# One Trainium2 core, a hybrid decoder layer: a hand-written TensorE order in which ten pieces of projection work instead of six stand ahead of the triangular solve's first product, and group norms that are issued in pieces

## The chip, the cores and the metric

One kernel runs on one core of a Trainium2 chip. A core has five engines with a queue of instructions each: TensorE (PE, matrix products; its weight loads are listed as PEld), VectorE (DVE), ScalarE (ACT), GpSimd (POOL) and SyncE (SP, which here only starts transfers). Each engine takes its instructions strictly in the order of its queue and waits on semaphores for other engines. The metric is the time of one execution on the device in microseconds (us), lower is better.

## What is computed

One decoder layer over 256 tokens of width 2048: RMSNorm, one input projection, whose columns go to two groups of heads, an output projection with a residual add, then a gated MLP of width 5632 with a causal convolution of three taps, and a final RMSNorm. Cut to what matters here, the two head groups are:

```python
def rwkv7_scan(r, w, k, v, a, b):            # 16 heads of 64, token by token
    sa = jnp.einsum('bhvk,bhk->bhv', state, a_t)
    state = state * w_t + sa[..., None] * b_t + v_t[..., None] * k_t
    out = jnp.einsum('bhvk,bhk->bhv', state, r_t)
...
mu = jnp.mean(y, axis=-1, keepdims=True)     # group norm of a head's 64 values
var = jnp.mean(jnp.square(y - mu), axis=-1, keepdims=True)
y = ((y - mu) * lax.rsqrt(var + GN_EPS)).reshape(bsz, s, c) * gn_w + gn_b
bonus = jnp.sum(r * k * r_k, axis=-1, keepdims=True) * v
return (y + bonus.reshape(bsz, s, c)) * g    # g: the gate
...
sc = q_nope @ k_nope.T + q_pe @ k_pe.T       # 8 attention heads, causal softmax, p @ v
```

## The kernel before

**Weights.** Every weight block of 128x1024 numbers is loaded by SyncE into a `raw` tile, ScalarE copies it to a rounded `hi` (L133) and VectorE writes the rest `lo` = raw - hi (L134); TensorE then multiplies hi by the activations' high and low parts and lo by their high part (`prod_c`, L175 and L178; `prod_a`, L195 to L197). Three buffers of each of raw, hi and lo go round. Accumulators in PSUM come from three rings: `mm` (3), `ch` (3) and `at` (2).

**The scan as a blocked solve.** The token-by-token recurrence is cut into four chunks of 64 tokens. For each head and chunk a triangular system of 64 is inverted by blocks of 32. `gram` (L525) forms the products, and its GpSimd transfers write the 32x32 blocks to a DRAM tile `dL`; `solve_load` (L578) reads them back as `Lp`; `solve` (L582) inverts the blocks on VectorE in 31 steps of a product `tm` (L594) and a sum `Tq` (L596) each, copies the result (`tp`, L598) and sends it by GpSimd transfers through DRAM into the tiles `T11` and `TT` (L604 to L613; the trace writes T11 as `T`). `solve_r` (L639) and `solve_t` (L654) then are 64 small 32x32 products each with the weight tiles T11 and TT; between them VectorE writes `RT`, after them `TT`. `chunk_a`, `chunk_b`, `chunk_c` (L697, L714, L723) do a chunk's products of state, solve and output, with VectorE evictions `XB`, `UV`, `ST` between them; the output lands in `yt`.

**The filling.** `all_units` (L917) is a generator of 30 pieces of projection work for the attention group, called units here: 16 halves of the eight latent tiles (two to a tile, `latent_tile`, L792; VectorE evicts a finished tile as `cr`, L801), then the up-projections (`up_b`, `up_v`). Behind the first latent tile of the second group, and again behind the first of the up-projections, stands a `latent_rs` (L814), which sends its sums `pss` through VectorE (`ssm`) and 14 small GpSimd instructions (`rsqrt`) to `rr`; `bcast` (L232) turns `rr` by two diagonal tiles `dg` and a product `rsb` into a row. `rope_q` (L846) rotates `qr` with a shifted copy `qs`, which four GpSimd transfers write.

**The order around the change.** From L969 on the order of TensorE's instructions is written out by hand (`manual_schedule`): `unit(6)`, `solve_r`, two units, `solve_t`, `chunk_a(0)`, two units, `chunk_b(0)`, a unit, `chunk_c(0)`, and for chunks 1 to 3 a unit before each of the three parts. Then come the eight attention heads: `scores(h)` (L870), the softmax on VectorE and ScalarE, `attend_t(h)` (L899, it waits for the softmaxed tile `pexp`) and `attend(h)` (L908), with the last units, the group norms of the two halves of the tokens (`gn_vec`, L746, `gn_gate`, L768, `gn_out`, L777) and the pieces of the output projection (`out_piece`, L952, 4 column blocks x 4 pieces for each half of the input) between them. The queues of the other engines are not written out: a scheduler places their instructions by its own model of time, and that order is fixed in the program. The rest of the program, from the output projection's second half through the MLP, lies behind that.

## Time and profile before

| what | value |
|---|---|
| runs shown | 6599.56, 1209.99 and 1216.69 us, median 1216.69 |
| the profiled execution | 1211.91 us, of which the span of the profile is 1210.1 us |
| TensorE busy over the span | 1164.1 us (96%) |
| VectorE, ScalarE, GpSimd busy | 815.7, 587.3 and 72.7 us |
| TensorE's mean granted clock | 0.986 |

The span is the time from the first to the last recorded instruction; the 1.8 us around it are not in the rows. A row of a timeline gives start, duration, engine, line, operation, output<-inputs and count; a bracket at its end is the idle time of that engine just before, with what ended it. A row of the waits gives who waited for whom, the total, the number of times and the longest. A row of the windows gives each engine's busy time in a stretch, TensorE's granted clock (1.00 is full) and the share and rate of the DMA engines. An x16 row of L175 or a x8 row of L178 is one half of a latent tile's three products.

### The profile page before, as it was taken

What the parts mean: (1) busy time and instruction counts of PE and PEld (TensorE: products, weight loads), DVE (VectorE), ACT (ScalarE), POOL (GpSimd) and SP (SyncE); (2) the same over time, 40 slices, a digit from 0 to 9 for tenths busy, and PEclk for the clock granted to TensorE, in tenths of its full rate; (3) what the DMA queues carried; (4) which work ended last, traced back from release to release, by engine and by line L of the source; (5) the groups of instructions that cost most, each with busy time, mean ns of one, the idle gap of its engine ahead of it and who ended that gap; (6) DMA issues with size and microseconds to landing.
All of it is one profiled execution on the core that took longest, in us unless ns stands there. A gap on an engine that the chain in (4) does not pass through costs nothing.

```text
span 1210.1 us, 19607 instructions
## 1 busy us (share of the span) xinstructions
PE 1164.1 (96%) x7629; PEld 1025.1 (85%) x7629; DVE 815.7 (67%) x1319; ACT 587.3 (49%) x895; POOL 72.7 (6%) x220
## 2 busy tenths in 40 slices
PE   7999989699998999999999999999999999999996
PEld 7899989598886788888888888888888888888885
DVE  6798669556687666777777776444577777776563
ACT  6684335234454345655555554333455555554442
POOL 1600430211000001000000000000000000000000
PEclk9999999789998999999999999999999999999998
DMA  8544455424332555655555555556655555566672
GB/s 323 201 141 156 132 166 174 134 95 145 122 125 92 187 188 175 194 191 191 191 191 191 191 192 191 190 189 192 205 191 191 191 190 191 190 222 208 209 213 83
DMA packets 61485, 215.90 MB, mean 178 GB/s; under 512 B 7376, under 2 KB 8144, under 8 KB 61392
## 3 DMA queue, kind: packets, MB, share of 16 engines
q1 hardware_dynamic: 58544, 209.22, 52.8%
q0 software_dynamic: 2080, 3.38, 1.0%
q10 hardware_dynamic: 768, 2.05, 0.6%
q8 instruction: 60, 0.98, 0.3%
q14 instruction: 33, 0.27, 0.1%
HBM read 210.48 MB, written 3.41 MB: 177 GB/s over the span
## 4 chain that ended last, share of the span: by engine, by line
PE 93%; DVE 3%; DMA 1%; issue 1%; ACT 1%; POOL 0%; ACTq 0%; SPq 0%; DVEq 0%
PE mm L163 27%; PE mm L166 13%; PE mm L175 12%; PE mm L195 9%; PE mm L197 9%; PE mm L196 9%; PE mm L178 6%; PE pg L538 1%; DVE lo L134 1%; PE px L691 1%; ACT hi L133 1%; PE at L175 1%; DMA raw<-in_win 0%; PE py L691 0%; PE pT L661 0%
## 5 line engine op out<-in xcount | busy, mean ns | idle before, releaser
L134 DVE TENSOR_TENSOR lo<-raw,hi 128x1024 fp32r<-128x1024 f32 x376 | 460.2, 1224 | 298.5 <-ACT hi L133 292.6
L133 ACT CAST hi<-raw 128x1024 fp32r<-128x1024 f32 x376 | 395.0, 1050 | 507.6 <-issue 230.6
L163 PE MATMUL mm<-z,hi 128*128 128x512 f32 x1408 | 351.3, 392 | 0.0
L163 PEld LDWEIGHTS mm<-z,hi 128*128 128x128 f32 x1408 | 251.9, 188 | 43.6
L166 PEld LDWEIGHTS mm<-z,lo 128*128 128x128 f32 x1408 | 188.3, 188 | 14.5
L166 PE MATMUL mm<-z,lo 128*128 128x256 f32 x1408 | 191.5, 278 | 0.0
L175 PE MATMUL mm<-x,hi 128*128 128x256 f32 x1024 | 143.0, 289 | 13.4 <-ACT hi L133 8.2
L175 PEld LDWEIGHTS mm<-x,hi 128*128 128x128 f32 x1024 | 130.7, 194 | 16.4 <-ACT hi L133 8.2
L196 PE MATMUL mm<-lo,hh 128*128 128x512 f32 x336 | 130.7, 389 | 0.0
L197 PE MATMUL mm<-hi,hl 128*128 128x512 f32 x336 | 130.7, 389 | 0.0
L195 PE MATMUL mm<-hi,hh 128*128 128x512 f32 x336 | 119.7, 389 | 0.0
L178 PE MATMUL mm<-x,lo 128*128 128x256 f32 x512 | 74.3, 282 | 0.0
L197 PEld LDWEIGHTS mm<-hi,hl 128*128 128x128 f32 x336 | 63.1, 188 | 13.1
L196 PEld LDWEIGHTS mm<-lo,hh 128*128 128x128 f32 x336 | 63.1, 188 | 13.1
L195 PEld LDWEIGHTS mm<-hi,hh 128*128 128x128 f32 x336 | 63.1, 188 | 13.0
L178 PEld LDWEIGHTS mm<-x,lo 128*128 128x128 f32 x512 | 66.1, 189 | 0.6 <-issue 0.3
L195 PE MATMUL mm<-hi,yhi 128*128 128x512 f32 x128 | 50.6, 403 | 1.3 <-DVE x L961 1.3
L197 PE MATMUL mm<-hi,ylo 128*128 128x512 f32 x128 | 50.5, 394 | 0.7 <-DVE ylo L914 0.7
L196 PE MATMUL mm<-lo,yhi 128*128 128x512 f32 x128 | 50.8, 397 | 0.0
L1098 POOL MEMSET gt<- 128x2 f32 x44 | 4.3, 99 | 577.0 <-DVE hl L1110 573.4
L195 PEld LDWEIGHTS mm<-hi,yhi 128*128 128x128 f32 x128 | 24.3, 190 | 7.8 <-DVE x L961 1.8
L197 PEld LDWEIGHTS mm<-hi,ylo 128*128 128x128 f32 x128 | 24.2, 189 | 6.5 <-DVE ylo L914 1.1
(283 smaller groups left out, 1103.6 us busy)
## 6 DMA issues: line engine op xcount, KB each, us to landing
raw<-in_wgu SPq DMA_DIRECT2D x176, 512.0 KB, 3.3
raw<-in_wdn SPq DMA_DIRECT2D x88, 512.0 KB, 4.2
raw<-in_win SPq DMA_DIRECT2D x70, 512.0 KB, 3.5
raw<-in_wout SPq DMA_DIRECT2D x32, 512.0 KB, 3.4
raw<-in_wuq SPq DMA_DIRECT2D x6, 512.0 KB, 3.3
xraw<-in_xT SPq DMA_DIRECT2D x4, 512.0 KB, 6.3
xt<-in_x SPq DMA_DIRECT2D x4, 512.0 KB, 6.9
raw<-in_wuk SPq DMA_DIRECT2D x4, 512.0 KB, 3.3
```

The lines of the kernel that those rows point to most:

```text
L133: S.copy(hi, raw)
L134: last_lo[0] = V.tensor_tensor(lo, raw, hi.bitcast(F32), ALU.subtract).ins
L163: PE.matmul(acc, hi[:, j * P:(j + 1) * P], act(kt0 + j), start=first and j == 0, stop=False, skip_group_check=True)
L166: PE.matmul(acc[:, :T], lo[:, j * P:(j + 1) * P], act(kt0 + j)[:, 0, :], start=False, stop=last and j == n - 1, skip_group_check=True)
L175: PE.matmul(acc, hi[:, j * P:(j + 1) * P], act(kt0 + j)[:, s, :], start=first and j == 0 and s == 0, stop=False, skip_group_check=True)
L178: PE.matmul(acc, lo[:, j * P:(j + 1) * P], act(kt0 + j)[:, 0, :], start=False, stop=last and j == n - 1, skip_group_check=True)
L195: PE.matmul(accs[tb], ah, wh, start=first and j == 0, stop=False)
L196: PE.matmul(accs[tb], ah, wl, start=False, stop=False)
L197: PE.matmul(accs[tb], al, wh, start=False, stop=last and j == n - 1)
L538: PE.matmul(pg[h][:, o:o + P], BK[pp][hs, gg, w * 2 + r, :, :], AR[pp][hs, gg, w * 2 + r, :, :], start=o == 0, stop=True, skip_group_check ...
L691: PE.matmul(dst[HS[h], a_ * 64:(a_ + 1) * 64], lhsT, rhs, start=first and n == 0 and a_ == 0, stop=True, skip_group_check=True)
L1098: nc.gpsimd.memset(gt[:, 0:2], 0.0)
```

## The change

What it does, part by part:

- `solve_load` starts its transfer on SyncE's queue, ahead of the next weight load, instead of GpSimd's; `solve` is issued after the second value tile instead of the first.
- In `solve_t` half of the copies into TT go to ScalarE.
- Ten units stand ahead of `solve_r` instead of six, `chunk_a(0)` follows `solve_r` directly, and one unit instead of two stands on either side of `solve_t`.
- `gn_vec` becomes a generator that is advanced between the heads; its bonus product and the add of the norm's offset go to GpSimd in a tile `bo` of its own (three instructions for each half of the tokens), where VectorE had four instructions (two products L763, and the adds L760 and L766) and now has one add.
- The heads' order: one unit between the early heads, all heads go through `step`, `out_piece(1, 0, 0)` stands ahead of head 3 and ahead of the last two units, `gn_out(0)` between heads 4 and 5, the first piece of the second column block between heads 6 and 7, and the second half's group norm behind head 7. The second column block takes its second accumulator from the ring `ch`.

```diff
--- before.py
+++ after.py
@@ -577,7 +577,8 @@
 
     def solve_load():
         Lps.append(sv("Lp").rearrange("p (i t) -> p i t", i=32))
-        nc.gpsimd.dma_start(Lps[0], dL)
+        with tc.issue_after(last_w[0]):
+            nc.sync.dma_start(Lps[0], dL)
 
     def solve():
         Lp = Lps[0]
@@ -623,7 +624,7 @@
         vt = []
         for g in range(2):
             vt.append(shifted(in_tile(17 + pp * 2 + g), 17 + pp * 2 + g))
-            if pp == 0 and g == 0:
+            if pp == 0 and g == 1:
                 solve()
         pt = ch("pv")
         for g in range(2):
@@ -662,7 +663,7 @@
                               TT[r0:r0 + 32, qq, 32:64], start=True, stop=True, tile_position=(r0, o0))
             for h in range(2):
                 o0 = h * 64
-                V.tensor_copy(TT[o0:o0 + 32, qh * 16:(qh + 1) * 16, 32:64],
+                (S.copy if h else V.tensor_copy)(TT[o0:o0 + 32, qh * 16:(qh + 1) * 16, 32:64],
                               pr_[o0:o0 + 32].rearrange("p (q s) -> p q s", q=16))
 
 
@@ -746,24 +747,32 @@
     def gn_vec(w):
         y = yt[w]
         y3 = y.rearrange("p (h v) -> p h v", h=16)
+        bo = s4(n="bo")
+        bq = bon.rearrange("p (r w a h) -> p r w a h", r=2, w=2, h=2)
+        for r in range(2):
+            nc.gpsimd.tensor_tensor(bo[HS[r]].rearrange("p (a h v) -> p a h v", a=8, h=2),
+                                    UV[w * 2 + r][0:64].rearrange("p a (h v) -> p a h v", h=2),
+                                    bq[:, r, w, :, :].unsqueeze(3).broadcast_to([64, 8, 2, 64]), ALU.mult)
+        nc.gpsimd.tensor_tensor(bo, bo, gnwb[1], ALU.add)
         mu = st("gmu", 16)
         V.tensor_reduce(mu, y3, AX.X, ALU.add)
         V.tensor_scalar(mu, mu, 1.0 / 64, None, ALU.mult)
+        yield
         V.tensor_tensor(y3, y3, mu.unsqueeze(2).broadcast_to([P, 16, 64]), ALU.subtract)
         sq = sv("gsq")
         S.activation(sq, y, AF.Square)
+        yield
         va = st("gva", 16)
         V.tensor_reduce(va, sq.rearrange("p (h v) -> p h v", h=16), AX.X, ALU.add)
+        yield
         rv = rsqrt(va, 1.0 / 64, GN_EPS, 16, V)
+        yield
         V.tensor_tensor(y3, y3, rv.unsqueeze(2).broadcast_to([P, 16, 64]), ALU.mult)
+        yield
         V.tensor_tensor(y, y, gnwb[0], ALU.mult)
-        V.tensor_tensor(y, y, gnwb[1], ALU.add)
-        bq = bon.rearrange("p (r w a h) -> p r w a h", r=2, w=2, h=2)
-        for r in range(2):
-            V.tensor_tensor(sq[HS[r]].rearrange("p (a h v) -> p a h v", a=8, h=2),
-                            UV[w * 2 + r][0:64].rearrange("p a (h v) -> p a h v", h=2),
-                            bq[:, r, w, :, :].unsqueeze(3).broadcast_to([64, 8, 2, 64]), ALU.mult)
-        V.tensor_tensor(y, y, sq, ALU.add)
+        yield
+        V.tensor_tensor(y, y, bo, ALU.add)
+        yield
 
     def gn_gate(w):
         y = yt[w]
@@ -951,7 +960,7 @@
 
     def out_piece(half, c, i):
         if i == 0:
-            oacc[c] = [mm() for _ in range(2)]
+            oacc[c] = [mm(), ch() if (half, c) == (1, 1) else mm()]
         if half == 1 and i == 2:
             load_x1(c)
         prod_a(oacc[c], piece(a["wout"][half, c, i]), lambda k: y_hl(yhi, half, k),
@@ -967,16 +976,18 @@
             next(units)
 
     with tc.manual_schedule(engines={mybir.EngineType.PE}):
-        unit(6)
+        unit(10)
         solve_r()
-        unit(2)
+        chunk_a(0)
+        unit()
         solve_t()
-        chunk_a(0)
-        unit(2)
+        unit()
         chunk_b(0)
         unit()
         chunk_c(0)
         for c in range(1, 4):
+            if c == 3:
+                gn = gn_vec(0)
             unit()
             chunk_a(c)
             unit()
@@ -991,49 +1002,55 @@
                 nc.scalar.dma_start(t, a[n].broadcast_to([P, 1024]))
             nc.scalar.dma_start(g2a, a["g2"][0:P])
             nc.scalar.dma_start(g2b[64:96], a["g2"][P:160])
-        def step(h, last=False):
+        def step(h, mid=None):
             attend_t(h)
             if h < 7:
                 scores(h + 1)
+            if mid:
+                mid()
             attend(h)
+            next(gn, None)
 
         scores(0)
-        unit(2)
+        next(gn)
+        unit()
+        next(gn)
+        unit()
         step(0)
-        unit(2)
-        attend_t(1)
         unit()
-        scores(2)
-        attend(1)
+        next(gn)
         unit()
+        step(1)
+        unit()
+        next(gn, None)
         step(2)
-        gn_vec(0)
-        unit(2)
-        attend_t(3)
         unit()
-        scores(4)
-        attend(3)
-        gn_gate(0)
+        next(gn, None)
+        out_piece(1, 0, 0)
+        step(3, lambda: gn_gate(0))
         unit()
+        unit()
+        assert next(units, None) is None
         step(4)
-        assert next(units, None) is None
-        out_piece(1, 0, 0)
+        out_piece(1, 0, 1)
+        gn_out(0)
         step(5)
-        out_piece(1, 0, 1)
+        out_piece(1, 0, 2)
         step(6)
-        gn_vec(1)
-        out_piece(1, 0, 2)
-        attend_t(7)
-        gn_out(0)
-        attend(7)
+        out_piece(1, 1, 0)
+        step(7)
         out_piece(1, 0, 3)
-        for c in range(1, 4):
+        for _ in gn_vec(1):
+            pass
+        for i in range(1, 4):
+            out_piece(1, 1, i)
+        for c in range(2, 4):
             for i in range(4):
                 out_piece(1, c, i)
-            if c == 1:
-                gn_gate(1)
-            if c == 2:
-                gn_out(1)
+                if (c, i) == (2, 2):
+                    gn_gate(1)
+                if (c, i) == (3, 1):
+                    gn_out(1)
 
 
     ssf = st("ssf", 8)
```

What that makes of VectorE's queue is shown at three places, with what it makes of GpSimd's. Numbers behind an underscore tell tiles of one name apart.

First place: VectorE where the solve begins. `lo` is a weight block's second part, `Lp` the solve's input, `tm` and `Tq` a step of it, `h` the eviction of an input-projection tile that frees its accumulator `mm`. Before:

```order
L134 TENSOR_TENSOR lo_2427<-raw_2424,hi_2426 128x1024
L590 TENSOR_TENSOR Lp_2046<-Lp_2046,Mp 128x1024
L594 TENSOR_TENSOR tm_2055<-Tq_2054,Lp_2046 128x31
L385 TENSOR_TENSOR h_2198<-mm_2137,rsB 128x256
L596 TENSOR_TENSOR Tq_2054<-Tq_2054,tm_2055 128x31
L385 TENSOR_TENSOR h_2274<-mm_2213,rsB 128x256
L594 TENSOR_TENSOR tm_2055<-Tq_2054,Lp_2046 128x60
```

and in the changed kernel:

```order
L134 TENSOR_TENSOR lo_2427<-raw_2424,hi_2426 128x1024
L134 TENSOR_TENSOR lo_2457<-raw_2454,hi_2456 128x1024
L591 TENSOR_TENSOR Lp_2046<-Lp_2046,Mp 128x1024
L595 TENSOR_TENSOR tm_2122<-Tq_2121,Lp_2046 128x31
L385 TENSOR_TENSOR h_2274<-mm_2213,rsB 128x256
L134 TENSOR_TENSOR lo_2503<-raw_2500,hi_2502 128x1024
L597 TENSOR_TENSOR Tq_2121<-Tq_2121,tm_2122 128x31
L385 TENSOR_TENSOR h_2341<-mm_2280,rsB 128x256
```

One more `lo`, that of the following weight block, stands ahead of the solve's input, and the eviction right behind it is that of the next tile (the eviction of the tile before has moved up, ahead of all these rows).

Second place: VectorE where the solve ends. `cr` is the eviction of a finished latent tile: `mm_2805` is the tile of units 5 and 6, `mm_2944` that of units 9 and 10. Before:

```order
L801 TENSOR_TENSOR cr_2866<-mm_2805,rsB 128x256
L134 TENSOR_TENSOR lo_3110<-raw_3107,hi_3109 128x1024
L596 TENSOR_TENSOR Tq_2054<-Tq_2054,tm_2055 128x28x4
L807 TENSOR_TENSOR css_2670<-css_2670,csq_2868 128x256
L810 SCALAR_TENSOR_TENSOR cl_2669<-cr_2866,vec,cl_2669 128x256
L594 TENSOR_TENSOR tm_2055<-Tq_2054,Lp_2046 128x87
L596 TENSOR_TENSOR Tq_2054<-Tq_2054,tm_2055 128x29x3
L594 TENSOR_TENSOR tm_2055<-Tq_2054,Lp_2046 128x60
L596 TENSOR_TENSOR Tq_2054<-Tq_2054,tm_2055 128x30x2
L594 TENSOR_TENSOR tm_2055<-Tq_2054,Lp_2046 128x31
L596 TENSOR_TENSOR Tq_2054<-Tq_2054,tm_2055 128x31
L598 COPY tp_2122<-Tq_2054 128x1024
```

and in the changed kernel:

```order
L810 TENSOR_TENSOR cr_3005<-mm_2944,rsB 128x256
L595 TENSOR_TENSOR tm_2122<-Tq_2121,Lp_2046 128x156
L134 TENSOR_TENSOR lo_3288<-raw_3285,hi_3287 128x1024
L597 TENSOR_TENSOR Tq_2121<-Tq_2121,tm_2122 128x26x6
L595 TENSOR_TENSOR tm_2122<-Tq_2121,Lp_2046 128x135
L597 TENSOR_TENSOR Tq_2121<-Tq_2121,tm_2122 128x27x5
L595 TENSOR_TENSOR tm_2122<-Tq_2121,Lp_2046 128x112
L597 TENSOR_TENSOR Tq_2121<-Tq_2121,tm_2122 128x28x4
L595 TENSOR_TENSOR tm_2122<-Tq_2121,Lp_2046 128x87
L597 TENSOR_TENSOR Tq_2121<-Tq_2121,tm_2122 128x29x3
L595 TENSOR_TENSOR tm_2122<-Tq_2121,Lp_2046 128x60
L597 TENSOR_TENSOR Tq_2121<-Tq_2121,tm_2122 128x30x2
```

In both the last steps of the solve stand behind the eviction of the very tile that TensorE finishes last ahead of `solve_r`: before from the step on 28 columns on, now from the step on 26. From the last row shown on there follow, before and now, the steps down to 31 values and then the copy `tp`.

Third place: VectorE around `bcast`. `rr` comes from GpSimd, `dg` are the two diagonals for TensorE's `rsb`, `qr` and `qs` the rotation, which needs the transfer of `qs`. Before:

```order
L821 TENSOR_SCALAR rr_3747<-ry_3749 128x2
L236 TENSOR_SCALAR dg_3918<-cst,rr_3747 128x128
L236 TENSOR_SCALAR dg_3921<-cst,rr_3747 128x128
L849 TENSOR_TENSOR qr_2654<-qr_2654,cosR 128x1024
L850 TENSOR_TENSOR qs_2655<-qs_2655,sinR 128x1024
L719 COPY UV_1920<-px_3807 64x4x64
```

and in the changed kernel:

```order
L830 TENSOR_SCALAR rr_3681<-ry_3683 128x2
L736 TENSOR_TENSOR ST_2645<-ST_2645,PC 64x4x64
L858 TENSOR_TENSOR qr_2654<-qr_2654,cosR 128x1024
L859 TENSOR_TENSOR qs_2655<-qs_2655,sinR 128x1024
L735 TENSOR_TENSOR ST_2646<-pS_3808,ST_2646 64x4x64 x2
L236 TENSOR_SCALAR dg_3842<-cst,rr_3681 128x128
L236 TENSOR_SCALAR dg_3845<-cst,rr_3681 128x128
L860 TENSOR_TENSOR qr_2654<-qr_2654,qs_2655 128x1024
L736 TENSOR_TENSOR ST_2646<-ST_2646,PC 64x4x64 x2
```

The diagonals, which stood ahead of the two rotation products, stand behind them and behind an update of the state `ST` now.

GpSimd's queue gets, right behind the transfers of `qs`, the six instructions of the bonus of both halves of the tokens, one behind the other:

```order
L857 DMA qs_2655<-qr_2654 32x1024 x4
L228 TENSOR_TENSOR ry_3683<-ry_3683,rt_3684 128x2
L753 TENSOR_TENSOR bo_4044<-UV_1917,bon 64x1024
L753 TENSOR_TENSOR bo_4044<-UV_1918,bon 64x1024
L756 TENSOR_TENSOR bo_4044<-bo_4044,gnb_4022 128x1024
L753 TENSOR_TENSOR bo_4644<-UV_1919,bon 64x1024
L753 TENSOR_TENSOR bo_4644<-UV_1920,bon 64x1024
L756 TENSOR_TENSOR bo_4644<-bo_4644,gnb_4022 128x1024
```

Before, the next instruction behind `ry` there was the root of the MLP's norm.

## The prediction

> **What bounds the kernel now.** I read the page's busy table first, then the windows, then TensorE's waits and, at the places they name, the timelines.
>
> ```profile
> span 1210.1 us, 19607 instructions
> PE 1164.1 (96%) x7629; PEld 1025.1 (85%) x7629; DVE 815.7 (67%) x1319; ACT 587.3 (49%) x895; POOL 72.7 (6%) x220
> ```
>
> TensorE sets the end, and the change takes no product away, so only TensorE's idle time and stretches at a low clock can be won or lost. The windows (length, then busy time of PE, PEld, DVE, ACT, POOL, then clock, DMA share, GB/s) tell how much that is.
>
> ```profile
> 150.00:392.50 242.50, 216.21 (x2230) 198.76 (x2229) 164.51 (x329) 100.96 (x185) 26.51 (x67) 0.94 0.41 131
> 392.50:1210.00 817.50, 808.04 (x4247) 691.39 (x4245) 534.08 (x733) 397.05 (x564) 8.09 (x58) 1.00 0.58 190
> 229.75:238.00 8.25, 7.82 (x150) 7.62 (x151) 2.76 (x4) 0.39 (x1) 1.92 (x3) 0.55 0.26 68
> 244.00:251.00 7.00, 7.00 (x88) 6.82 (x86) 4.23 (x9) 0.00 (x0) 0.00 (x0) 0.51 0.21 73
> 316.00:367.80 51.80, 48.34 (x293) 40.48 (x292) 38.20 (x82) 26.83 (x56) 0.00 (x0) 0.99 0.37 123
> 367.80:374.00 6.20, 6.18 (x20) 5.35 (x21) 1.21 (x6) 1.83 (x6) 0.00 (x0) 0.52 0.26 85
> ```
>
> The instructions that move lie between about 150 and 392.5 us. There TensorE is idle for 242.50 - 216.21 = 26.3 us, and three stretches at about half clock lose up to 8.25 x 0.45 + 7.00 x 0.49 + 6.20 x 0.48 = 10.1 us. So 36 us, 3.0% of the span, is the most that any order could win. Its waits from 150 to 425 us (who waited for whom: total, times, longest) name the idle time:
>
> ```profile
> PE pR L646 <- DMA T<-dU: 11.7, 2, 11.3
> PE mm L175 <- DVE Tq L596: 3.3, 1, 3.3
> PE ptp L904 <- DVE pexp L894: 3.2, 2, 2.9
> PE pS L691 <- DVE ST L734: 3.0, 2, 1.9
> PE mm L195 <- DVE x L961: 1.3, 1, 1.3
> PE py L691 <- DVE UV L719: 1.2, 2, 0.6
> PE py L691 <- DVE ST L737: 0.8, 1, 0.8
> PE mm L197 <- DVE ylo L914: 0.7, 1, 0.7
> PE psc L879 <- DVE kn L844: 0.6, 1, 0.6
> PE po L911 <- ACT pT L905: 0.3, 1, 0.3
> ```
>
> The largest is the gap ahead of `solve_r`, 11.3 us. The four units that move ahead of it are to fill it.
>
> **Term 1, where the solve starts.** TensorE's and VectorE's rows:
>
> ```profile
> 177.21 2.06 PE L175 MATMUL mm<-x,hi 128*128 128x256 f32 x16 [3.31 <-DVE Tq L596]
> ...
> 174.07 1.22 DVE L134 TENSOR_TENSOR lo<-raw,hi 128x1024 fp32r<-128x1024 f32 x1 [1.60 <-ACT hi L133]
> 175.21 1.22 DVE L590 TENSOR_TENSOR Lp<-Lp,Mp 128x1024 f32<-128x1024 f32 x1
> 176.64 0.42 DVE L385 TENSOR_TENSOR h<-mm,rsB 128x256 f32<-128x256 f32 x1
> ```
>
> The tile at 177.21 needs an accumulator that the eviction `h` frees, and `h` stands behind `Lp`. In the changed order this eviction stands ahead of `Lp`, and the one behind `Lp` is for the next tile, two half-tiles later (about 4 us at 2.06 each), with one more `lo` (1.22) and `Lp` ahead of it. That leaves a wait of about 0.5. Term 1 is -2.8, with bounds 0 (the wait only moves a tile on) and -3.3.
>
> **Term 2, the gap ahead of `solve_r`.** The first product behind the gap, and VectorE's end of the solve:
>
> ```profile
> 229.75 0.28 PE L646 MATMUL pR<-T,G 32*32 32x32 f32 x2 [11.28 <-DMA T<-dU]
> ...
> 215.63 0.32 DVE L594 TENSOR_TENSOR tm<-Tq,Lp 128x156 f32<-128x156 f32 x1
> 218.52 0.42 DVE L801 TENSOR_TENSOR cr<-mm,rsB 128x256 f32<-128x256 f32 x1 [0.22 <-PE mm L178]
> 220.51 0.48 DVE L810 SCALAR_TENSOR_TENSOR cl<-cr,vec,cl 128x256 fp32r<-128x256 f32 x1
> 222.47 1.03 DVE L598 COPY tp<-Tq 128x1024 f32<-128x1024 f32 x1
> ```
>
> The gap is two parts. From the start of `cr` to the end of `tp` VectorE takes 223.50 - 218.52 = 5.0 us; from there the transfers through DRAM take 229.75 - 223.50 = 6.25 us. More units ahead of `solve_r` cover this only if the solve runs on while they run. It does not: the queue is in order, and `cr` there waits for the tile that TensorE finishes last. In the changed order the `cr` of units 9 and 10 stands in that place, with five more step instructions behind it than before (156, 156, 135, 135 and 112 values; 0.32 each by the row above, 1.6 in all) and without `css` and `cl` between (0.35 to 0.4 each, 0.7). VectorE has done all the earlier steps and stands idle till unit 10 ends, as it stood for 0.22 before 218.52. So four units run ahead, 4 x 3.0 us of work that was due anyway, and the gap comes behind them as long as before plus 0.9: about 12.2 us, `solve_r` near 239. Term 2 is +0.9; bounds -11.7 (whole wait gone) and +2 (each added step behind another `lo`).
>
> **Term 3, half clock behind the gap.** Before, 229.75 to 238 and 244 to 251 run at 0.55 and 0.51. The gap stays, so these stay; `solve_r`, the products of `chunk_a`, a unit, `solve_t` and another unit are the same work in another order, within half a row of 0.9 us. +0.4; bounds -7 (the clock holds, two thirds of the 10.1) and +3 (one more stretch as long as the last of them). The copies given to ScalarE in `solve_t` cost nothing: VectorE and ScalarE together are busy for 4.23 of the 7.00 us there, under TensorE's 7.00.
>
> **Term 4, the four chunks.** The rotation and `rsb` around 305 us:
>
> ```profile
> 305.62 0.48 DVE L236 TENSOR_SCALAR dg<-cst,rr 128x128 f32<-128x128 f32 x2
> 308.11 1.23 DVE L849 TENSOR_TENSOR qr<-qr,cosR 128x1024 f32<-128x1024 f32 x1 [2.00 <-DMA qs<-qr]
> 309.25 1.22 DVE L850 TENSOR_TENSOR qs<-qs,sinR 128x1024 f32<-128x1024 f32 x1
> 306.84 0.71 PE L237 MATMUL rsb<-dg,ones 128*128 128x128 f32 x4
> ```
>
> Before, `dg` was written at once and the `UV` copies stood behind the rotation, which waits for the transfer of `qs`. Now a pair of `ST` sums and `dg` stand behind it. `dg` would be there at 309.25 + 1.22 + 0.9 (the pair) + 0.25 (half of 0.48) = 311.6 on the clock of before. TensorE comes to `rsb` behind the same two units, with the parts b and c of a chunk between instead of a and b, some 0.4 us later: 307.2. So a new wait of 4.4. The waits for `ST` (0.8 and 3.0) stay; those for `UV` (1.2) and `kn` (0.6, two more units now lie ahead of the first head) go. (0.8 + 3.0 + 4.4) - (0.8 + 3.0 + 1.2 + 0.6) = +2.6. Bounds: -1.8 (no new wait) and +5.6 (the new wait also halves the clock, which at 367.80 cost 3.0).
>
> [...]
>
> **Term 5, the heads.** Before, their waits are 3.2 + 1.3 + 0.7 + 0.3 = 5.5 (`pexp`, `x`, `ylo`, `pT`), and 3.0 at half clock (6.20 x 0.48) behind the longest. Its row, with the softmax's last two steps on ScalarE and VectorE:
>
> ```profile
> 365.93 0.45 ACT L889 ACTIVATE pexp<-psc,mx,rr 128x128 f32<-128x128 f32 x1
> 367.39 0.55 DVE L894 TENSOR_SCALAR pexp<-pexp,sm 128x128 f32<-128x128 f32 x2
> 367.82 0.88 PE L904 MATMUL ptp<-cst,pexp 128*128 128x128 f32 x3 [2.92 <-DVE pexp L894]
> ```
>
> This was head 5's softmax, behind a block of `gn_vec` and `gn_gate` on VectorE that the change takes apart, so the wait and its low clock should go. But in ScalarE's changed queue head 2's exponential stands behind both `qn` copies of the unit ahead of `attend_t(2)`, and has no cover then: 367.39 + 0.55 - 365.93 = 2.0, with the copy before it 2.3. Two units ahead of head 4 find one free accumulator of three, since `out_piece(1, 0, ...)` holds two: twice 0.5 for the eviction and 1.05 for its product. And four short waits of 0.1 to 1.25 for ScalarE's copies, 2.35 in all. 2.3 + 2.05 + 2.35 = 6.7 against 8.5: -1.8. Bounds -8.5 and +3 (a second low stretch).
>
> **Term 6, the bonus on GpSimd.** VectorE's pair of products, and the nearest GpSimd rows (the second groups eight by minimum, median and maximum in ns):
>
> ```profile
> 349.93 2.44 DVE L763 TENSOR_TENSOR gsq<-UV,bon 64x1024 f32<-64x1024 f32 x2
> L621 POOL MEMSET UV<- 64x1024 f32 x4 | 3.6, 948 | 0.1
> L304 POOL TENSOR_SCALAR sinR<-rp x8: 358/374/1416, 30.5 to 39.5; 32x64 f32<-32x64 f32 x8
> 477.69 1.23 DVE L134 TENSOR_TENSOR lo<-raw,hi 128x1024 fp32r<-128x1024 f32 x1 [0.78 <-ACT hi L133]
> ...
> 477.70 1.26 POOL L222 TENSOR_TENSOR rt<-ry 128x2 f32<-128x2 f32 x1
> 298.66 0.19 POOL L213 TENSOR_SCALAR rm<-ssm 128x2 f32<-128x2 f32 x1 [36.18 <-DVE ssm L819]
> ```
>
> The group norms now have six GpSimd instructions of 1024 columns: not under 0.95 each (the memset, which reads nothing), not over 2.9 (0.36 for 64 columns, of which 0.19 is the floor, by the row at 298.66: 0.17 / 64 x 1024 + 0.2). I take 2.4, nearer to the row that computes: 14.4 in all. VectorE loses three 1.22 instructions for each half, 7.3 in all. But beside a `lo` of VectorE a 0.2 us GpSimd instruction takes 1.26, as long as the `lo` itself: one of the two stands still. So VectorE may stand still for up to 14.4 us. It is busy for 38.20 of 51.80 us in this stage; in the 13.6 free, and the 3.7 more of its own that go there, most finds room. I count +2.5 where a softmax waits just then; bounds 0 and +14.4.
>
> [...]
>
> **The sum.** -2.8 + 0.9 + 0.4 + 2.6 - 1.8 + 2.5 = +1.8. The profiled execution took 1211.91 us, so the forecast is **1213.7 us**: no change. The runs shown lie at 1209.99 and 1216.69 (their median; 0.55% apart), so this profile is 4.8 under the median, and a measurement tells about 2%, 24 us, from no change.
>
> **The rivals.**
> - The filling works: the solve ends under the four units, gap and low clock go. -11.7 - 7 + 0.4 for the order instead of terms 2 and 3: 1211.9 - 18.3 - 2.8 + 2.6 - 1.8 + 2.5 = 1194. For it speaks that four units, 12 us, are just as long as the gap; against it the `cr` of unit 10 ahead of twelve step instructions. Chance 0.10.
> - The heads' waits go, their low stretch too, and GpSimd's work is free: 1213.7 - 6.7 - 2.5 = 1204.5. For it: VectorE loses its block of group norm. Against: head 2's exponential behind the copies. Chance 0.17.
> - Slower: GpSimd's lock. All six instructions fall where VectorE's `pexp` or `lo` is what TensorE waits for, as `pexp` was at 367.82: 1213.7 - 2.5 + 14.4 = 1225.6. It decides where VectorE has less than 2.4 us to spare, as a GpSimd instruction starts, before the next thing that TensorE waits for. For it the stretched row at 477.70; against it the 13.6 us free. Chance 0.15.
> - The forecast: 0.58, by itself 1207 to 1220.
>
> **How the numbers follow.** The range reaches from between the two faster rivals, 1200 (0.05 below), to the slower one, 1226 (0.08 above). Faster by over 2% means under 1192.4 beside the median, the near half of the first rival's spread: 0.05. Slower by over 2%, over 1241, needs the lock and low clocks at once: 0.03.
>
> **What would show it.** Right: the wait of `pR` for `T` stays near 12, the row of `mm` for `Tq` near 0.5; a new wait of 4 for `dg` at `rsb`; the GpSimd rows of the bonus near 2.4 each, VectorE's instructions beside them stretched; the stretch behind the heads as before. Wrong: `pR` waiting for less than 6, no low clock behind it, or waits for `pexp` of over 10 us in all.

## The result, and the profile after

The changed kernel takes 1220.88 us (median of 20 runs, 1216.51 to 1227.01) against 1216.9 for the kernel before: a ratio of 1.0041, with a 95% interval of 1.0023 to 1.0058. It is slower by 4 to 5 us, clear of noise and well inside 2%. The forecast of 1213.7 was "no change" with the sum at +1.8, and its range held the time. But the forecast lay 3 us under the median of the kernel before and the time lies 4 us over it, and the sign of the heads in the sum was wrong. The profiled execution took 1221.73 us, of which 1219.9 are the span. Single executions of several thousand us, like the 6599.56 of the kernel before, are left out of all ratios.

TensorE's waits in the changed kernel, in the stretch from 150 to 425 us (who waited for whom, total, times, longest):

```profile
PE pR L647 <- DMA T<-dU: 12.8, 2, 12.4
PE ptp L913 <- DVE pexp L903: 6.6, 2, 4.7
PE rsb L237 <- DVE dg L236: 5.1, 1, 5.1
PE pS L692 <- DVE ST L735: 3.0, 2, 1.9
PE mm L175 <- ACT qn L851: 1.4, 2, 1.0
PE po L920 <- ACT pT L914: 1.4, 2, 1.2
PE mm L175 <- DVE h L385: 1.3, 1, 1.3
PE py L692 <- DVE ST L738: 0.8, 1, 0.8
PE mm L175 <- DVE kn L853: 0.5, 1, 0.5
```

The gap ahead of `solve_r` is still the first row, 12.4 against 11.3. `rsb` waiting for `dg` is new, and `pexp` has doubled from 3.2. The waits for `Tq`, `UV`, `x` and `ylo` are gone. The windows by stage (length, busy time of PE, PEld, DVE, ACT, POOL, then the clock, the DMA engines' share and GB/s) show what stands behind the waits:

```profile
242.20:253.90 11.70, 11.19 (x189) 10.77 (x189) 4.61 (x9) 0.84 (x1) 4.47 (x17) 0.55 0.20 48
300.00:312.00 12.00, 5.83 (x82) 5.45 (x81) 8.89 (x16) 2.69 (x6) 0.00 (x0) 0.81 0.38 115
312.00:326.00 14.00, 14.00 (x202) 12.12 (x201) 5.74 (x10) 4.56 (x7) 4.54 (x2) 0.92 0.23 76
326.00:353.00 27.00, 20.93 (x137) 18.46 (x135) 24.90 (x43) 15.23 (x32) 10.66 (x4) 0.98 0.48 161
353.00:362.00 9.00, 8.26 (x43) 7.58 (x44) 3.32 (x13) 2.60 (x7) 0.00 (x0) 0.69 0.19 60
```

The first is `solve_r` and what follows it, at half clock as before (0.55 in both). The next two are the new wait at `rsb` and a lowered clock behind it: at most 12 x 0.19 + 14 x 0.08 = 3.4 us lost, of which 2.8 in the 6.0 us right behind the wait (308.7 to 314.7 us, clock 0.54), where TensorE had work throughout. The fourth is heads 0 to 2, where VectorE is busy for 24.90 of 27.00 us; the last is the low clock behind the wait of 4.7 there (9 x 0.31 = 2.8).

From `solve_r` to the first head's scores the two profiles take 83.9 and 83.4 us, the second with two units fewer (2.83 each): +5.2. From there to the MLP it is 160.5 and 158.3, again with two units fewer, now as up-projections: +3.5. Behind that both take 735.9. Ahead of 150 us, where no part of the change lies, the changed kernel is already 2.1 us behind: the same row of products `pg` starts at 140.91 before and at 143.06 now, and between 30 and 60 us the clock was 1.00 before and 0.94 now (30 x 0.06 = 1.8). So of the 9.8 us between the two spans about 7.7 can be due to the change.

### The profile page after: what moved, and what is told of

Its sections match the earlier page's. It is cut to its first block, busy times and chain, and to the rows that moved or that the text cites. A ratio compares the mean times of both kernels' runs of the same rounds, so it can differ in the third digit from the quotient of the medians.

```text
span 1219.9 us, 19610 instructions
## 1 busy us (share of the span) xinstructions
PE 1167.5 (96%) x7629; PEld 1029.4 (84%) x7629; DVE 814.2 (67%) x1311; ACT 588.7 (48%) x897; POOL 85.2 (7%) x225
## 4 chain that ended last, share of the span: by engine, by line
PE 68%; DVE 0%; ACT 0%; issue 0%; ACTq 0%
PE mm L163 26%; PE mm L166 13%; PE mm L195 9%; PE mm L196 9%; PE mm L197 9%; PE pxT L1069 0%; PE mm L175 0%; PE pgate L783 0%; PE po L920 0%; PE psc L890 0%; PE psc L888 0%; PE pgate L782 0%; PE ch L196 0%; PE ch L197 0%; PE ch L195 0%; PE pyT L791 0%
## 5 line engine op out<-in xcount | busy, mean ns | idle before, releaser
L196 PE MATMUL mm<-lo,yhi 128*128 128x512 f32 x120 | 47.4, 395 | 0.0
L197 PE MATMUL mm<-hi,ylo 128*128 128x512 f32 x120 | 47.1, 393 | 0.0
L195 PE MATMUL mm<-hi,yhi 128*128 128x512 f32 x120 | 46.9, 399 | 0.0
L175 PE MATMUL mm<-cl,hi 128*128 128x256 f32 x160 | 25.5, 306 | 2.0 <-ACT qn L851 1.4
```

What stands on the lines that cost most here:

```text
L175: PE.matmul(acc, hi[:, j * P:(j + 1) * P], act(kt0 + j)[:, s, :], start=first and j == 0 and s == 0, stop=False, skip_group_check=True)
L195: PE.matmul(accs[tb], ah, wh, start=first and j == 0, stop=False)
L196: PE.matmul(accs[tb], ah, wl, start=False, stop=False)
L197: PE.matmul(accs[tb], al, wh, start=False, stop=last and j == n - 1)
```

## The experiments

A ratio is to the runs of the kernel before on the same chip, beside them; an interval that holds 1 is no difference. In the profiles of the single runs waits and stretches are compared, not totals, since the total moves by several us with the clock (1206.4 us at 0.991 to 1219.0 at 0.978, last section). "Gap" is the wait of `pR` for `T` ahead of `solve_r`.

### Why the four units did not fill the gap

The prediction said that the solve's last steps stand behind `cr` of the tile that TensorE finishes last, and that VectorE is idle till then. The changed kernel's VectorE there, rows of its timeline:

```profile
229.15 0.34 DVE L597 TENSOR_TENSOR Tq<-Tq,tm 128x175 f32<-128x175 f32 x1
229.93 0.42 DVE L810 TENSOR_TENSOR cr<-mm,rsB 128x256 f32<-128x256 f32 x1 [0.44 <-PE mm L178]
230.27 0.31 DVE L595 TENSOR_TENSOR tm<-Tq,Lp 128x156 f32<-128x156 f32 x1
```

It is idle for 0.44 us. In the whole solve up to unit 10's end it works nearly all the time, as the same stretch of both kernels shows (changed kernel first):

```profile
181.20:230.30 49.10, 47.42 (x403) 47.04 (x401) 45.04 (x92) 27.95 (x43) 0.29 (x3) 1.00 0.57 177
```

```profile
175.20:218.50 43.30, 41.27 (x350) 41.10 (x350) 40.50 (x89) 25.05 (x41) 0.39 (x4) 1.00 0.52 161
```

The load of its input, and the first instruction on it, in the changed kernel:

```profile
162.59 12.60 SPq L127 DMA_DIRECT2D raw<-in_win  x5
175.50 0.33 SPq L581 DMA_DIRECT2D Lp<-dL  x1
```

```profile
181.19 1.23 DVE L591 TENSOR_TENSOR Lp<-Lp,Mp 128x1024 f32<-128x1024 f32 x1 [0.70 <-DMA Lp<-dL]
```

Before, the solve had 43.30 us until TensorE's last unit ended; with four units more it has not 11.3 but 5.8 more. It starts at 181.2 instead of 175.2, which is 3.9 later beside the 2.1 by which the whole profile is late, and TensorE's wait inside the stretch is 2.0 shorter (1.27 for 3.31). The experiments that follow settle what that means.

**`e5_late_cr`** takes the eviction out of the solve's way:

```diff
-        V.tensor_copy(tp, Tq.rearrange("p s t -> p t s"))
+        stp[0] = V.tensor_copy(tp, Tq.rearrange("p s t -> p t s")).ins
...
-        V.tensor_tensor(cr, acc[:, :T], rsB, ALU.mult)
+        with tc.issue_after(stp[0] if (x, j) in ((0, 3), (1, 0)) else last_lo[0]):
+            V.tensor_tensor(cr, acc[:, :T], rsB, ALU.mult)
```

> The changed kernel with the evictions cr of the tiles of units 7 to 10 issued behind the solve's copy tp, so that no solve step stands behind an eviction that waits for TensorE's last units. The prediction's theory, that this place in VectorE's queue alone keeps the solve from running on under the units: gap ahead of solve_r down from 12.4 to 4 or less, time near 1210. Rival, that VectorE has no time left (45.0 of the 49.1 us between the solve's start and unit 10's end are busy in the changed kernel's profile): the gap shrinks by what is taken out of VectorE's way, 2 to 4 us, to some 9, time near 1218.

The gap was 11.4, the ratio 1.0055 (1.0032 to 1.0078). With `cr` away the gap lost 1.0 us, no more, and the time did not fall. The place in the queue was not what held the solve. The rival's direction is right, its size (2 to 4) too large.

**`e6_start`** undoes the solve's start:

```diff
-        with tc.issue_after(last_w[0]):
-            nc.sync.dma_start(Lps[0], dL)
+        nc.gpsimd.dma_start(Lps[0], dL)
...
-            if pp == 0 and g == 1:
+            if pp == 0 and g == 0:
                 solve()
```

> The changed kernel with the solve's start as before: its load on GpSimd's queue and solve issued after the first value tile. Theory of the start: in the changed profile Lp begins at 181.2 instead of 175.2, and these 6 us on a nearly full VectorE are what eats the four units; with the old start tp ends near 225.5, so that the gap is 2 to 3 us, the low clock behind it shrinks, the wait of 3.3 at 177 comes back, and the time is near 1209. The prediction's theory of the place behind the last cr: gap 11 to 13, time near 1221.

`tp` ended at 225.2, while TensorE's units ran until 229.4, and the gap fell to 6.3 us. So the start was what kept the solve on VectorE from ending under the units: the theory holds for VectorE. It fails for the rest. The ratio was 1.0038 (1.0014 to 1.0062), as for the changed kernel, and the gap did not fall to 2. Its window ahead of `solve_r` tells why:

```profile
229.00:236.00 7.00, 0.66 (x6) 0.35 (x4) 1.56 (x2) 0.98 (x2) 3.79 (x5) 0.79 1.01 287
```

The DMA engines are full (1.01, 287 GB/s). The solve's transfers took 235.7 - 225.2 = 10.5 us beside weight loads, the last 6.7 of them in this window, and 6.3 us in the kernel before, where TensorE stood still and no weight load ran beside them (share 0.56 from 223.5 to 229.75 us). The gap on VectorE turned in part into one on the transfers. That the weight loads make them longer is argued from these shares and not tested: VectorE, which did nothing during the transfers before, works for 4.59 of the 10.5 us here, and no run parts the two.

**`e12_load_pool`, `e13_place`, `e14_start10`, `e10_start12`** part the two halves of the start, on a base without the two other costs (`e9_front_dg`, below). The edits are the one half or the other of the diff above, both, and both with `unit(12)` and two units fewer between heads.

> As e9_front_dg, but the solve's load stands on GpSimd's queue again; solve still behind the second value tile. If the load's late landing alone (issued at 175.5 on SyncE behind weight loads, landed at 181.2) delays the solve: Lp begins 4 to 6 us earlier against the tiles and the gap falls to 7 or less. Rival, that the place in VectorE's queue holds it at the second value tile anyway: Lp at most 1 earlier, gap 12 to 13, time within 2 of e9_front_dg.

> As e9_front_dg, but solve is issued behind the first value tile again; the load stays on SyncE. VectorE then stands at Lp from about 176 until the load lands near 181, and TensorE's tile behind an eviction waits with it: a wait of 6 to 9 for Tq or h where e9 has 1.1, tp some 4 us earlier than in e9 against the units, gap 7 to 9; time within 3 of e9_front_dg. Rival, that SyncE's load lands in time: wait under 4 and gap 6, time 3 to 5 under e9.

> As e10_start12 with ten units instead of twelve: the front of before for the solve's load and place, dg ahead of the rotation, heads and group norms of before. In e6_start the gap was 6.3 with a low clock behind it. Theory that the gap's length counts: 2 to 4 us slower than e10_start12, near 1213. Rival, that what twelve units win in the gap is lost again in the 5.6 us that TensorE stood in the products behind it while the transfers filled all DMA engines: within 1.5 of e10_start12.

> As e9_front_dg, and the solve's load and place as before, with twelve units ahead of solve_r (and two fewer between heads). tp ended at 225.2 in e6_start, and its transfers took 10.5 us beside weight loads: about 236. Twelve units end near 235. Theory of the start: gap under 2, full clock behind it, time 10 or more under before, near 1204. Rival, that the transfers take as much longer as more weight loads run beside them: gap 4 to 8, time 1209 to 1213.

| kernel | solve's start to the last unit's end, us | wait for `Tq` or `h` | gap | ratio (95%) |
|---|---|---|---|---|
| `e9_front_dg`: as the change | 232.6 - 183.8 = 48.8 | 1.1 | 12.6 | 0.9969 (0.9942 to 0.9997) |
| `e12_load_pool`: load on GpSimd | 228.9 - 180.2 = 48.7 | 0.5 | 12.0 | 0.9973 (0.9953 to 0.9993) |
| `e13_place`: behind the first value tile | 235.3 - 179.3 = 56.0 | 5.3 | 6.9 | 0.9990 (0.9969 to 1.0011) |
| `e14_start10`: both | 231.4 - 175.1 = 56.3 | 3.3 | 6.0 | 0.9977 (0.9956 to 0.9998) |
| `e10_start12`: both, twelve units | 238.3 - 177.7 = 60.6 | 3.3 | none | 0.9947 (0.9924 to 0.9970) |

The place behind the second value tile sets the start; the load on SyncE, started behind a row of weight loads and landed 5.7 us later, adds a stall once the place is early. In `e12_load_pool` the rival came out. In `e13_place` the theory did, by its gap and its time, with a shorter wait than it had (5.3 for 6 to 9); behind the gap of 6.9 `solve_r` waits for `T` a second time, 2.2 us. But a gap of 6 instead of 12 does not show in the time: 0.9969 and 0.9977 are not apart. Of the 6.6 us won, 2.2 go back at the wait for `Tq` (3.3 for 1.1), and in `e14_start10` the products behind the gap are slow for longer, which costs 2.2 more: the same products, from the second row of `pR` to the unit behind `solve_t`, take 258.65 - 238.50 = 20.15 us, for 263.69 - 245.74 = 17.95 in `e9_front_dg`; what is left is within the noise.

`e14_start10` against `e10_start12` stays open: the medians are 0.8 us apart, as its rival had it, the ratios 3.0 thousandths, as its theory had it, and the intervals overlap. With twelve units the gap is gone, but the next products stall, as `e10_start12`'s timeline and window have it:

```profile
247.79 1.12 PE L693 MATMUL px<-UV,G 128*64 128x64 f32 x14 [5.62 <-issue]
```

```profile
235.50:247.00 11.50, 5.95 (x171) 5.52 (x169) 6.38 (x9) 1.21 (x2) 6.89 (x18) 0.83 1.00 215
247.00:262.00 15.00, 14.21 (x183) 13.90 (x184) 3.59 (x6) 2.20 (x3) 0.00 (x0) 0.61 0.13 39
```

Half of the gap is back as 5.6 us in the middle of `chunk_a(0)`, with the DMA engines full (1.00), and the low clock is back behind it (0.61). The 1209.78 us were some 5 above the 1204 of the theory and in the rival's 1209 to 1213, but the rival's gap of 4 to 8 did not come either; the stall came in its place.

### The wait at `rsb`

**`e8_dg`** issues the rotation behind `dg`:

```diff
+    def rotate():
+        with tc.issue_after(last_dg[0]):
-        V.tensor_tensor(qr, qr, cosR.unsqueeze(1).broadcast_to([P, 4, T]), ALU.mult)
+            V.tensor_tensor(qr, qr, cosR.unsqueeze(1).broadcast_to([P, 4, T]), ALU.mult)
...
         bcast(rrs[1], rrB1, mm, t2)
+        rotate()
```

`last_dg` is the second diagonal of `bcast`; the other two instructions of the rotation follow in `rotate` as well.

> The changed kernel with the rotation of qr and qs issued behind dg on VectorE instead of ahead of it. If the place of dg in the queue makes the new wait at rsb: the wait falls from 5.1 to 1 or less, and the low clock behind it (0.81 and 0.92 in the next two stages) goes, time 4 to 6 under the changed kernel, near 1215. Rival, that TensorE then waits for the same transfer a step later (UV or the first head's qr): the wait at rsb goes and one of 2 to 4 for UV or qr comes, time within 2 of the changed kernel.

The row of TensorE in the changed kernel and in `e8_dg`:

```profile
308.70 1.22 PE L237 MATMUL rsb<-dg,ones 128*128 128x128 f32 x4 [5.10 <-DVE dg L236]
```

```profile
305.31 0.71 PE L239 MATMUL rsb<-dg,ones 128*128 128x128 f32 x4 [1.63 <-DVE dg L238]
```

The wait fell to 1.6, no other came in its place, and the four products took 0.71, as in the kernel before at a clock of 1.00, not 1.22. Ratio 0.9988 (0.9969 to 1.0006): 6 us under the changed kernel, of which 3.5 are the wait. Behind it the products are not slowed (the 32 `px` at 314.71 take 1.15 us, as in the kernel before at 254.98 at a clock of 1.00), where the changed kernel lost about 2.8 us. From `solve_r` to the first head it was 75.9 us instead of 83.4. The theory holds; only the wait that is left is longer than the 1 expected.

### The heads

**`e1_front`** is the change's front with the heads and group norms of before, **`e2_heads`** the reverse; since two more or fewer units are left for the heads, two `unit(2)` behind `scores(0)` and head 0 became `unit()` in the first, and the reverse in the second. **`e9_front_dg`** is `e1_front` with the edit of `e8_dg`.

> The changed kernel with the heads of before: gn_vec whole and on VectorE, the old order of heads and output pieces, one unit instead of two behind scores(0) and behind head 0, since two more units have gone ahead. From the two profiles the part up to the first head costs about +4.3 us (start of the solve -2.0, gap +1.1, chunks and clock +5.2), the heads +3.5. If the costs add: gap ahead of solve_r 12.4 as in the changed kernel, wait at rsb near 5, time near 1221 against 1217 for before, no GpSimd bonus. Rival, that the heads alone carry the loss: time within 1 of before.

> The kernel before with the changed heads, group norms in pieces and GpSimd bonus; two units instead of one in the two places behind scores(0), to use up the two units that have not gone ahead. If the costs add: gap 11.3 as before, no wait at rsb, waits for pexp of 3 to 6 in all, time near 1220. Rival, that VectorE is held by GpSimd only because of the later front: pexp waits under 3 and time near 1217.

> The front of the change with the heads and group norms of before (as e1_front) and dg ahead of the rotation. If the two costs found so far add up, this is e1_front less the wait at rsb: gap 12.3, rsb under 1, time 3 to 5 under before, near 1212. Rival, that the wait only moves on: near 1216 as e1_front.

`e1_front` came to 1.0010 (0.9986 to 1.0033), with the gap of 12.2 and the wait of 5.2 at `rsb`: the change's front by itself is not told from no change, so that beside the kernel before the loss is in the heads, as its rival had it. `e9_front_dg` was 1211.73 us, 0.9969: the time as expected, the wait at `rsb` 1.6 for under 1. So the front wins about as much elsewhere as it loses at `rsb`. `e2_heads` was 1.0060 (1.0035 to 1.0084), but it does not price the heads alone: in its order GpSimd's bonus falls ahead of `rsqrt`, so that `rr` is late (317.88) and `rsb` waits 7.7:

```profile
300.90 3.94 POOL L752 TENSOR_TENSOR bo<-UV,bon 64x1024 f32<-64x1024 f32 x2 [34.99 <-PE py L691]
305.93 1.15 POOL L213 TENSOR_SCALAR rm<-ssm 128x2 f32<-128x2 f32 x1 [1.09 <-DVE ssm L827]
307.16 2.38 POOL L755 TENSOR_TENSOR bo<-bo,gnb 128x1024 f32<-128x1024 f32 x1
```

Its wait for `pexp` was one of 2.5, on the side of its rival (under 3). There the pieces stand in the heads too, but two more units cover them and half of the bonus is done before the heads begin, so that this run does not part the causes.

What the heads wait for stands in the changed kernel's rows of VectorE, GpSimd and TensorE:

```profile
332.88 3.07 DVE L134 TENSOR_TENSOR lo<-raw,hi 128x1024 fp32r<-128x1024 f32 x1
336.21 2.59 DVE L134 TENSOR_TENSOR lo<-raw,hi 128x1024 fp32r<-128x1024 f32 x1
...
346.50 1.22 DVE L770 TENSOR_TENSOR yt<-yt,ry 128x1024 f32<-128x1024 f32 x1
347.64 1.22 DVE L134 TENSOR_TENSOR lo<-raw,hi 128x1024 fp32r<-128x1024 f32 x1
348.78 0.61 DVE L894 TENSOR_REDUCE mx<-psc 128x1 f32<-128x128 f32 x2
349.31 1.21 DVE L772 TENSOR_TENSOR yt<-yt,gnw 128x1024 f32<-128x1024 f32 x1
350.44 0.41 DVE L923 TENSOR_TENSOR ylo<-po,yhi 128x256 fp32r<-128x256 f32 x1
350.78 0.15 DVE L895 TENSOR_TENSOR mx<-mx,rr 128x2 f32<-128x2 f32 x1
350.84 1.22 DVE L774 TENSOR_TENSOR yt<-yt,bo 128x1024 f32<-128x1024 f32 x1
```

```profile
332.18 2.69 POOL L756 TENSOR_TENSOR bo<-bo,gnb 128x1024 f32<-128x1024 f32 x1 [11.88 <-DMA gnb<-in_gnb]
334.83 5.73 POOL L753 TENSOR_TENSOR bo<-UV,bon 64x1024 f32<-64x1024 f32 x2
340.64 2.36 POOL L756 TENSOR_TENSOR bo<-bo,gnb 128x1024 f32<-128x1024 f32 x1
```

```profile
343.37 0.61 PE L913 MATMUL ptp<-cst,pexp 128*128 128x128 f32 x3 [1.86 <-DVE pexp L903]
353.74 0.87 PE L913 MATMUL ptp<-cst,pexp 128*128 128x128 f32 x3 [4.72 <-DVE pexp L903]
```

Two things are in the softmax's way. Beside GpSimd's instructions two `lo` take 3.07 and 2.59 us instead of 1.22 (the prediction's lock, an instruction of VectorE that takes longer beside one of GpSimd's: here by 1.85 and 1.37 us). And pieces of the group norm (`yt` by `ry`, `gnw`, `bo`) stand ahead of and between the steps of head 2's softmax (`mx` to `pexp`).

**`e3_bonus_dve`** takes the lock away and leaves the pieces:

```diff
-        for r in range(2):
-            nc.gpsimd.tensor_tensor(bo[HS[r]].rearrange("p (a h v) -> p a h v", a=8, h=2),
...
-        nc.gpsimd.tensor_tensor(bo, bo, gnwb[1], ALU.add)
...
         V.tensor_tensor(y, y, gnwb[0], ALU.mult)
+        V.tensor_tensor(y, y, gnwb[1], ALU.add)
         yield
+        for r in range(2):
+            V.tensor_tensor(bo[HS[r]].rearrange("p (a h v) -> p a h v", a=8, h=2),
```

> The changed kernel with its group norms in pieces and its order of heads, but the bonus and the offset's add back on VectorE, behind the multiplication with the norm's weight. In the changed profile two loads' lo of VectorE beside GpSimd's bonus take 3.07 and 2.59 instead of 1.22, and TensorE waits for pexp 1.86 at head 1 and 4.72 at head 2. Theory of the lock: the stretched lo go, pexp waits fall from 6.6 to under 3, time 3 to 4 under the changed kernel (1217). Rival, that the group norm's pieces themselves stand ahead of the softmax on a VectorE that is over 90% busy there: the lo are short again but the pexp waits stay at 6 or grow, since VectorE has 3.7 us more to do, time 1220 to 1223.

The stretched `lo` are 1.22 again, the waits for `pexp` 5.4 in place of 6.6, one of 1.8 for `ylo` is new, and the ratio is 1.0040 (1.0020 to 1.0061), that of the changed kernel. The rival holds by its time, with waits a little under its 6: taking the lock away wins nothing if VectorE gets the 3.7 us of work back. What the lock costs by itself this run does not tell.

**`e16_gn_only`** moves the pieces, and nothing else, and **`e11_gn_late`** does it with the edit of `e8_dg`; in **`e17_gn_dve`** the bonus stands on VectorE again, in **`e15_best`** the solve's start is that of before.

```diff
         step(2)
+        for _ in gn_vec(0):
+            pass
         unit()
-        next(gn, None)
         out_piece(1, 0, 0)
```

The other calls of `next(gn)`, from `scores(0)` on, are left out.

> The changed kernel with nothing undone but the place of the first half's group norm, which is issued whole behind head 2; dg stays behind the rotation. If the two costs are separate and add: the pexp waits fall as in e11_gn_late to about 1, the wait at rsb stays at 5, time 8 under the changed kernel, near 1213 against 1215.5 for before. Rival, that either alone keeps the heads or the clock low: time within 3 of the changed kernel, 1218 or more.

> As e8_dg (the changed kernel with dg ahead of the rotation), but the first half's group norm is issued whole behind head 2, where it stood before the change, and not in pieces from scores(0) on; its bonus stays on GpSimd. If the pieces on VectorE ahead of the softmax of heads 1 and 2 make the heads dear: the pexp waits there go from 6.6 to under 2.5, a wait of up to 3 comes at a later head as before the change, time 3 to 4 under e8_dg, near 1212. Rival, that the single unit and ScalarE's queue make them: pexp at head 2 stays over 4 and time stays near 1215.

> As e11_gn_late with the bonus and the offset's add on VectorE instead of GpSimd: what the move to GpSimd is worth by itself. In e11_gn_late VectorE's lo beside GpSimd's bonus still take 2.77 and 4.53 for two, and TensorE waits for pexp only 1.0. If the lock costs something: this one is 1 to 3 faster than e11_gn_late. Rival, that VectorE's own 3.7 us for each half weigh more than standing still where nothing waits for it: 1 to 4 slower than e11_gn_late.

> As e11_gn_late with the solve's load and place as before the change: all three repairs together. If the shorter gap counts beside the other two: gap near 6 instead of 12.3, a wait of 3.3 for Tq, time 2 to 5 under e11_gn_late, near 1203. Rival, that as between e9_front_dg and e14_start10 the won gap does not show in the time: within 1.5 of e11_gn_late.

| kernel | `rsb` | `pexp` | gap | us | ratio (95%) |
|---|---|---|---|---|---|
| the change | 5.1 | 6.6 | 12.4 | 1220.88 | 1.0041 (1.0023 to 1.0058) |
| `e8_dg` | 1.6 | 6.6 | 12.5 | 1214.99 | 0.9988 (0.9969 to 1.0006) |
| `e16_gn_only` | 5.4 | 1.1 | 12.3 | 1214.49 | 0.9988 (0.9969 to 1.0007) |
| `e11_gn_late`: both | 1.6 | 1.0 | 12.3 | 1206.97 | 0.9943 (0.9921 to 0.9965) |
| `e17_gn_dve`: both, bonus on VectorE | 1.6 | 0.6 | 12.6 | 1209.50 | 0.9958 (0.9936 to 0.9980) |
| `e15_best`: both, solve's start of before | 1.6 | 1.4 | 6.2 | 1207.07 | 0.9927 (0.9898 to 0.9956) |

Each repair alone takes 0.0053 off the ratio, both 0.0098: the two costs are separate and all but add, as `e16_gn_only` was to tell. The row of the waits in `e16_gn_only`, beside the 6.6 of the changed kernel:

```profile
PE ptp L913 <- DVE pexp L903: 1.1, 1, 1.1
```

`e11_gn_late` is faster than expected (1206.97 for 1212); the wait of up to 3 that was to come at a later head did not, which is part of the difference. And it keeps the lock:

```profile
335.70 1.21 DVE L900 TENSOR_TENSOR mx<-mx,rr 128x2 f32<-128x2 f32 x1
...
339.14 4.53 DVE L134 TENSOR_TENSOR lo<-raw,hi 128x1024 fp32r<-128x1024 f32 x2
```

```profile
334.01 4.85 POOL L755 TENSOR_TENSOR bo<-UV,bon 64x1024 f32<-64x1024 f32 x2
338.95 2.50 POOL L758 TENSOR_TENSOR bo<-bo,gnb 128x1024 f32<-128x1024 f32 x1
```

VectorE's `lo` still take longer beside GpSimd's bonus (4.53 us for two), and even a `mx` of 0.15 takes 1.21, yet TensorE waits 1.0 us for `pexp` in all heads: with the pieces gone VectorE has time to spare (busy for 21.14 of 27.70 us from 324.3 to 352.0). `e17_gn_dve`, without a lock, is not faster; it is 1.5 thousandths slower, within the intervals. That is the side of its rival. `e15_best` has the lowest ratio of all, 0.9927 from six runs, but is not told apart from `e11_gn_late`: the gap is 6 us shorter, 2.5 go back at the wait for `Tq` (3.3 for 0.8), and what is left does not show clearly. It beats both kernels, the one before by 0.7%.

## Why the prediction was wrong

- **Term 1** (-2.8): the wait was 1.27, not 0.5, so -2.0. The mechanism is right; the load's landing at 181.2 holds `Lp` 0.7 longer than the sum had it.
- **Term 2** (+0.9): +1.1, a gap of 12.4 for the 12.2 forecast. The size is right by luck and the reason wrong. "VectorE has done all the earlier steps and stands idle till unit 10 ends" fails: it was idle for 0.44 us, and with `cr` out of the way the gap lost 1.0. What ate the units is the solve's start, 3.9 us later against the same work by its place behind the second value tile, on a VectorE that is 92% busy, and the 2.0 us of wait that term 1 won. The prediction had the late start in term 1 and did not carry it into term 2.
- **Term 3** (+0.4): half clock came back behind the gap, as forecast, but in one stretch and not in two. It lost 11.7 x 0.45 = 5.3 us, for 8.25 x 0.45 + 7.00 x 0.49 = 7.1 before: -1.8. Why the second stretch stayed away no run tells.
- **Term 4** (+2.6): the new wait was 5.1 for 4.4, and `UV` went as forecast, so +3.3 on the waits. The mechanism is right. Mis-sized is the clock behind it, which stood only in the bound: about 2.8 us were lost there, +6.1 in all. Undoing the order took 6 us off.
- **Term 5** (-1.8): the step that failed. The waits are 6.6 + 1.4 + 1.4 + 0.5 = 9.9 for 6.7 forecast, with 2.8 at a low clock behind the longest, against 8.5 in all before: +4.2. The prediction took the group norm in pieces as out of the way and saw only ScalarE's copies ahead of head 2's softmax (2.3). In fact seven pieces moved to heads 0 to 2, where VectorE was then busy for 24.90 of 27.00 us. Moving them back alone takes 6 us off, and the waits for `pexp` fall from 6.6 to 1.1.
- **Term 6** (+2.5): the price of one instruction was right (2.3 to 2.9 each, 15.4 in all for 14.4), and the lock shows in `lo` of 3.07 and 2.59 us for 1.22. The cost on the path did not show: with the bonus on VectorE the kernel is no faster, with or without the pieces, so that the move as a whole is put at 0 here. In `e11_gn_late`, where VectorE had time to spare (6.56 of 27.70 us), the stretched rows left TensorE only 1.0 us of waiting for `pexp`.

With these sizes the sum is 1.8 + 0.8 + 0.2 - 2.2 + 3.5 + 6.0 - 2.5 = +7.6 (the six terms put right), beside the 7.7 between the two spans from 150 us on. So the sum missed by term 5 above all, which has the wrong sign, then by the clock in term 4. The step that failed is in term 5: that the group norm, once in pieces, is out of the softmax's way.

The forecast missed by its starting point as well. It lies 1220.88 - 1213.7 = 7.2 us under the result, and 5.0 of these are the 1211.91 from which the sum started, one execution that was 5.0 under the median of 1216.9. The prediction had seen that it was low and started from it all the same; from the median that it showed, 1216.69, the same sum would have given 1218.5, slower as measured, though still with the wrong heads in it. For the same reason the medians lie only 4 apart and the two profiled executions 9.8.

The signs that the prediction named spoke for it in the main: `pR` near 12, the wait for `dg`, the price of the bonus, and `pexp` under 10 in all. None of them would have shown heads that lose 4 us.

The rival "the heads' waits go" fails, since `pexp` doubled. The rival "slower: GpSimd's lock" had the right side but the wrong mechanism. The rival "the filling works" fails with the start, and with the old start it fails in half on the transfers.

## What to carry to other kernels

Work that is issued ahead of a wait fills it only if what is waited for runs on meanwhile: ask whether its engine has time left and whether its start moved, before asking what stands in its queue. A long chain of side work cut into pieces does not get out of the way of a short urgent chain when the engine is full at that place (VectorE was busy for 24.90 of 27.00 us); the same pieces behind head 2 left 1.1 us of waiting for `pexp` in place of 6.6. The waits of 4.7 and 5.1 us on TensorE cost more than their length here, since the clock behind them fell (to 0.69 and 0.54). And a sum of terms is added to the median of several executions, not to the one that was profiled.

## What the runs showed of the hardware

- TensorE's waits of 4.7 and 5.1 us were followed by a clock of 0.69 (353 to 362 us) and 0.54 (308.7 to 314.7 us), and taking away 3.5 us of the longer one gave 6 us. These traces show no sharp length: before the change 2.9 us ahead of 367.82 were followed by a clock of 0.52 (367.8 to 374.0 us) and 3.3 ahead of 177.21 by one of 1.00 (177.2 to 183.2 us), and the products `pS` behind the same wait of 1.9 took 0.69 us before and 1.12 after.
- The granted clock differs from one execution to the next: among 33 of the kernel before on one chip, spans of 1206.4 at 0.991 and of 1219.0 at 0.978. Span times clock is 1195.5 and 1192.2, so that most of the spread goes with the clock, and one profile's total, as the 1211.91 that the sum started from, may lie 5 us off the median (1216.9).
- The solve's transfers, of 32x32 blocks through DRAM, took 6.0 to 6.5 us while TensorE stood still (6.03 in `e2_heads`, 6.25 before the change, 6.38 with it, 6.53 in `e5_late_cr`) and 10.4 and 10.2 in `e6_start` and `e10_start12`, where weight loads and VectorE's instructions ran beside them.
- In `e10_start12` TensorE stood for 5.6 us in the middle of 32 like products, for nothing that the profile shows, while the DMA engines were full (1.00 from 235.5 to 247 us). Four packets of the instruction queue are among the transfers from 222 to 262 us; whether TensorE stood for its next instructions no run tested, and it is left open.
